# Attention of a hybrid backbone: where the norm's sums, the direct group and the last output products stand in the order

## The chip, the cores and the metric

The kernel runs on one core of one Trainium2 chip. The metric is device microseconds per execution; lower is better. Before the change, three runs gave 2841.94, 2845.85 and 2846.23 us, a median of 2845.85.

## The reference

The computation is a backbone of two layers over 1024 latent tokens and 256 context tokens of width 1024. Layer 0 mixes tokens by differential attention (8 heads, two score maps of 64 dimensions each, values of 128), layer 1 by a bidirectional state-space layer. Every mixer is followed by a squared-ReLU MLP of width 4096. All in float32. The change lies in the attention:

```python
def attend(q, k, v):
    s = jnp.einsum('bqhcd,bkhcd->bhcqk', q, k).astype(jnp.float32)
    p = jax.nn.softmax(s, axis=-1)
    w = p[:, :, 0] - lam * p[:, :, 1]
    o = jnp.einsum('bhqk,bkhe->bqhe', w.astype(v.dtype), v)
    return rmsnorm(o, subln_g) * (1.0 - lambda_init)
...
y_lat = jnp.einsum('bte,ed->btd', o_l, w_o)
```

Latent queries read all 1280 keys, context queries only the 256 context keys.

## The kernel before

**Number format.** A float32 product is made of three matmuls of rounded halves (hi·hi, hi·lo, lo·hi: `mm3`, L132, L133, L134). An operand is split by ScalarE (ACT), which writes the rounded hi half (L137), and by VectorE (DVE) or GpSimd (POOL), which writes the rest, lo (L138).

**Units.** Attention is the function `phase_b`. It runs 8 heads of 9 units, n = 9·head + u, and then a tail of five steps, n = 72 to 76. Unit u = 0 holds the 256 context queries, units 1 to 8 hold 128 latent queries each. Two latent units form a pair; the context unit is pair 0, so a head has five pairs, 0 to 4. A unit's scores wait for one another in this chain: scores on PE (L579, 18 matmuls), the two maps' maxima with a copy out of PSUM on DVE (L592), two exponentials on ACT (L602), and the combination of the two maps on DVE (L610, L611, L613). In the following unit the combined weights are transposed on PE in three parts (L625; L620 behind a context unit) and split, either straight from PSUM (`w_direct`: ACT L631 for hi, DVE L632 for lo) or by way of a copy (`w_copy`: ACT L638, then POOL L641 and L642). When a pair is complete, PE multiplies its weights with the values, ACT copies the result out (L732), POOL squares it (L733), and PE sums the squares over the head's 128 dimensions with a column of ones (`pair_sums`, L740); ACT copies the sums (L741).

**Fills.** Beside this chain PE has the projections of the next head's queries and keys. A group of them is eight products of three matmuls into bank 7 (in head 7, six products of the output matrix W_o). The table `FILLS` says how many stand ahead of the unit's first transposes, behind them, and behind the combination. Groups end either directly (ACT L523, DVE L524: hi and lo out of PSUM) or with the rotary embedding (ACT L528, DVE L529, POOL L534, DVE L537, and a split). In unit 2 the group has a direct end only, in the rows called `now`.

**PSUM.** There are eight banks of 512 columns. Scores of the first map take columns 0 to 1279 (banks 0, 1 and half of 2), of the second 1792 to 3071 (from the last quarter of bank 3 to bank 5). Columns 1280 to 1791, halves of banks 2 and 3, are called `whole` and take transposes. Bank 6 is `pb`: its lower half takes the values' products, its upper half (`high`) or the whole (`low`) takes transposes. Bank 7 takes the fills.

**Norms.** The sums of heads 0 to 6 are made into factors one head later (L746 to L748 on DVE, a transpose of the factors L760 to columns 1280 to 1407, L774 on DVE). Head 7 has no head behind it, so each of its pairs is normed by itself (`norm7`): factors on DVE and POOL (L746 to L748, L144), a diagonal matrix on POOL (L810), its broadcast by a matmul with ones (L814), a multiplication on DVE (L816) and a split. The steps of `norm7` are taken up at the ends of the two units behind the sums.

**W_o.** The output's first 512 columns for all ten token tiles start inside head 7 and the tail: a group takes six of the eight slices k of the contraction and is stored to `wod` in HBM (L857 copies it from PSUM). The last two slices, k = 6 and 7, of seven tiles are taken at n = 74, in the banks of the table `WO_BANKS`; later DVE adds them to what comes back from `wod` (L1453). The weights of these slices are split by `wsplit6(3)`: ACT L137 and POOL L138 of 1024 columns.

**What sets the order.** In `phase_b` the order on PE, DVE, ACT and POOL is the order in which the program writes the instructions (`manual`). SyncE's queue (SP) issues the loads and stores. What follows attention (the rest of W_o in `phase_c`, the MLP, layer 1) is ordered by a scheduler that lists the instructions by its own estimates, and is listed anew for a changed program.

Of the kernel before, what the change touches and what calls it, by code (L numbers as in the profile page):

```python
# [70 lines left out]
class Prog:  # L71
# [581 lines left out]
    FILLS = {0: (0, 3, 5, 8), 1: (0, 0, 0, 8), 2: (0, 2, 8, 8)}  # L653
# [28 lines left out]
    def phase_b(self):  # L682
# [24 lines left out]
        pb = self.bank(6)  # L707
# [29 lines left out]
        def pair_sums(h, pair):  # L737
            b = pb[:, 0:2] if h == 7 and pair > 2 else self.PS[:, 1790:1792]
            for i in range(2):
                mm(b[:, i : i + 1], sq[:, 128 * i : 128 * i + 128], self.ones, start=True, stop=True)  # L740
            nc.scalar.activation(hst[:, 1, h, 2 * pair : 2 * pair + 2], b, AF.Copy)  # L741
# [60 lines left out]
        def norm7(pair):  # L802
            b = pb[:, 256:512]
            newton = norm_calc(7, 2 * pair, 2 * pair + 2)
            g, c0 = cols7[pair]
# [55 lines left out]

        wo_at = dict(zip((63, 64, 65, 66, 68, 69, 70, 71, 72, 73), [8, 9] + list(range(8))))
# [15 lines left out]
        with self.manual():  # L878
            for n in range(72 + 5):
                h, u = units[n] if n < 72 else (8, 9)  # L880
                front = n < 72
                groups = []
# [24 lines left out]
                if groups:  # L907
                    a = self.FILLS.get(u, (0, 1, 5, 8) if n < 63 else (0, 0, 4, 6) if late else (0, 1, 4, 6))
                    if n > 71:
                        a = (0, 2, 4, 6) if n == 72 else (0, 4, 6, 6)  # L910
                    fills = [groups[0][0][a[i] : a[i + 1]] for i in range(3)]
# [69 lines left out]
                else:  # L981
# [14 lines left out]
                    w1 = part(1, last[:, 256:512] if pv and h < 7 else self.bank(0)[:, 0:256] if n == 72 else high)  # L996
# [5 lines left out]
                    now = groups and n < 63 and len(groups[0][1]) == 1  # L1002
                    if now:
                        groups[0][1][0]()
# [8 lines left out]
                if split:  # L1013
                    split()
                todo7, run7 = run7, []
# [23 lines left out]
                if n in (58, 61, 62, 70):  # L1039
                    wsplit6((58, 61, 62, 70).index(n))  # L1040
# [5 lines left out]
                if n == 74:  # L1046
                    for i, j in self.WO_BANKS.items():
                        g = 2 if i > 7 else i // 4
                        c0 = 128 * (i - self.G_TILES[g][0])
                        for k in (6, 7):  # L1050
                            hh, hl = (t[:, k, c0 : c0 + 128] for t in self.oT[g])
                            self.mm3(self.bank(j), hh, hl, wt6[k][0], wt6[k][1], k == 6, k == 7)
# [1593 lines left out]
```

## Time and profile before

| quantity | value |
| --- | --- |
| runs | 2841.94, 2845.85, 2846.23 us |
| profiled execution: time | 2845.55 us |
| profiled execution: span | 2843.8 us |
| PE busy | 2713.8 us, 95% of the span |
| DVE busy | 2025.9 us, 71% |
| ACT busy | 1368.1 us, 48% |
| POOL busy | 978.9 us, 34% |
| attention (`phase_b`) | 219 to 881 us of the span |

Times in rows of the profile are microseconds from the span's start, unless they are marked as ns. A row of the timeline gives the start, the duration, the engine, the line, the operation, the written and read buffers, their shapes, the count of equal instructions that follow one another, and, in brackets, how long the engine was idle before it and whose end it waited for. A row of the groups gives the same for all instructions of a line: the busy time, the mean of one in ns, then the idle time before them with what ended it.

### The profile page before, as it was taken

What the parts mean: (1) busy time and instruction counts of PE and PEld (TensorE: products, weight loads), DVE (VectorE), ACT (ScalarE), POOL (GpSimd) and SP (SyncE); (2) the same over time, 40 slices, a digit from 0 to 9 for tenths busy, and PEclk for the clock granted to TensorE, in tenths of its full rate; (3) what the DMA queues carried; (4) which work ended last, traced back from release to release, by engine and by line L of the source; (5) the groups of instructions that cost most, each with busy time, mean ns of one, the idle gap of its engine ahead of it and who ended that gap; (6) DMA issues with size and microseconds to landing.
All of it is one profiled execution on the core that took longest, in us unless ns stands there. A gap on an engine that the chain in (4) does not pass through costs nothing. (4 is left out here: it accounts for less than half of the span.)

```text
span 2843.8 us, 43784 instructions
## 1 busy us (share of the span) xinstructions
PE 2713.8 (95%) x15645; PEld 2259.5 (79%) x15645; DVE 2025.9 (71%) x3024; ACT 1368.1 (48%) x2584; POOL 978.9 (34%) x822
## 2 busy tenths in 40 slices
PE   5999999999999999999999999789999999999999
PEld 4688888888777787788877788788887778888887
DVE  6367888888773676767798877899543697668466
ACT  3425556666553753333444445477444633344443
POOL 3314555566553600000030013688121143335414
PEclk9999999999999999999999999899999999999999
DMA  9944233333515358886799877579642244477544
GB/s 273 322 170 138 62 89 92 94 91 110 167 58 175 130 186 313 296 308 215 258 312 304 279 232 260 171 231 307 229 163 89 71 161 159 154 246 228 167 132 141
DMA packets 377448, 539.13 MB, mean 190 GB/s; under 512 B 38287, under 2 KB 231053, under 8 KB 374029
## 3 DMA queue, kind: packets, MB, share of 16 engines
q1 hardware_dynamic: 377228, 536.32, 58.1%
q8 instruction: 123, 2.02, 0.3%
q14 instruction: 97, 0.79, 0.1%
HBM read 367.54 MB, written 164.47 MB: 187 GB/s over the span
## 5 line engine op out<-in xcount | busy, mean ns | idle before, releaser
L132 PE MATMUL PS<-H 128*128 128x512 f32 x1072 | 421.0, 394 | 2.5 <-ACT H L137 1.8
L134 PE MATMUL PS<-H 128*128 128x512 f32 x1072 | 418.0, 391 | 2.9 <-DVE H L138 1.6
L133 PE MATMUL PS<-H 128*128 128x512 f32 x1072 | 418.1, 390 | 0.0
L132 PE MATMUL PS<-H,R 128*128 128x512 f32 (+1 forms) x828 | 308.2, 374 | 12.5 <-DVE R L524 9.0
L133 PE MATMUL PS<-H,R 128*128 128x512 f32 (+1 forms) x828 | 299.1, 361 | 0.0
L134 PE MATMUL PS<-H,R 128*128 128x512 f32 (+1 forms) x828 | 298.3, 361 | 0.0
L132 PEld LDWEIGHTS PS<-H 128*128 128x128 f32 x1072 | 201.3, 188 | 50.3 <-issue 6.2
L134 PEld LDWEIGHTS PS<-H 128*128 128x128 f32 x1072 | 201.3, 188 | 46.0 <-DVE H L138 2.4
L133 PEld LDWEIGHTS PS<-H 128*128 128x128 f32 x1072 | 201.4, 188 | 40.4
L132 PE MATMUL PS<-R,H 128*128 128x512 f32 x534 | 213.7, 401 | 5.3 <-ACT H L137 3.3
L137 ACT ACTIVATE R<-W 128x512 fp32r<-128x512 f32 (+1 forms) x185 | 129.6, 708 | 179.1 <-PE PS L133 104.9
L137 ACT ACTIVATE H<-U 128x640 fp32r<-128x640 f32 x216 | 131.9, 675 | 173.2 <-PE PS L133 145.1
L133 PE MATMUL PS<-R,H 128*128 128x512 f32 x534 | 210.8, 395 | 2.8 <-POOL R L138 2.8
L134 PE MATMUL PS<-R,H 128*128 128x512 f32 x534 | 211.4, 397 | 1.8 <-DVE H L138 1.8
L602 ACT ACTIVATE F<-F,stat 128x1280 f32<-128x1280 f32 x128 | 174.3, 1362 | 80.3 <-DVE F L592 80.3
L592 DVE TENSOR_SCALAR_CACHE_REDUCE F<-PS 128x1280 f32<-128x1280 f32 x128 | 185.2, 1483 | 22.5 <-PE PS L579 22.5
L138 DVE TENSOR_TENSOR H<-U,H 128x640 fp32r<-128x640 f32 x216 | 162.2, 785 | 50.9 <-ACT H L137 50.6
L138 DVE TENSOR_TENSOR H<-W,H 128x512 fp32r<-128x512 f32 (+1 forms) x137 | 124.5, 919 | 102.0 <-ACT H L137 101.5
L132 PEld LDWEIGHTS PS<-H,R 128*128 128x128 f32 x828 | 157.6, 191 | 42.5 <-DVE R L524 10.4
L137 ACT ACTIVATE H<-W 128x512 fp32r<-128x512 f32 (+2 forms) x158 | 95.2, 613 | 186.3 <-PE PS L133 121.5
L134 PEld LDWEIGHTS PS<-H,R 128*128 128x128 f32 x828 | 157.4, 190 | 25.1 <-issue 0.8
L133 PEld LDWEIGHTS PS<-H,R 128*128 128x128 f32 x828 | 157.8, 191 | 19.8
(530 smaller groups left out, 6708.1 us busy)
## 6 DMA issues: line engine op xcount, KB each, us to landing
W<-in_mlp_w SPq DMA_DIRECT2D x176, 256.0 KB, 3.4
U<-Aa SPq DMA_DIRECT2D x108, 320.0 KB, 4.4
Aa<-FU SPq DMA_DIRECT2D x91, 320.0 KB, 4.7
Ad<-F SPq DMA_DIRECT2D x112, 256.0 KB, 2.9
W<-Ad SPq DMA_DIRECT2D x112, 256.0 KB, 2.7
FU<-in_mlp_w SPq DMA_DIRECT2D x32, 512.0 KB, 6.1
Ta<-FU SPq DMA_DIRECT2D x16, 1024.0 KB
U<-in_ada_w SPq DMA_DIRECT2D x32, 512.0 KB, 9.8
```

What stands on the lines that cost most here:

```text
L132: mm(out, ah, bh, start=first, stop=False, **kw)
L133: mm(out, ah, bl, start=False, stop=False, **kw)
L134: mm(out, al, bh, start=False, stop=last, **kw)
L137: self.nc.scalar.activation(hi, src, AF.Copy)
L138: (lo_eng or self.nc.vector).tensor_tensor(lo, src, hi.bitcast(F32), ALU.subtract)
L592: ts(p[c], self.PS[:, 1792 * c : 1792 * c + 1280], 1.0, None, ALU.mult, ALU.min, accum_out=sm[:, c : c + 1])
L602: nc.scalar.activation(p[c], p[c], AF.Exp, bias=sm[:, c : c + 1], scale=-1.0, accum_out=sn[:, 0:1] if c else s0[:, u + 1 : u + 2])
```

## The change

Six places are rewritten. None adds or removes an instruction on an engine.

1. The fills' table: in unit 0 four products (before, three) stand ahead of the first transposes and two behind them; unit 3 gets a row of its own, with two products ahead of them and five behind. In head 7, units 0 takes 4, 0 and 2 of W_o's six products, and units 3 to 8 have 2, 2 and 2 (or 0, 4 and 2) for 1, 3 and 2 (or 0, 4 and 2).
2. The sums of pair 4, which are made in unit 1 of the next head, go to columns 0 and 1 of bank 6, not to the last two columns of `whole` in bank 3.
3. In unit 2 the direct end of the projection group stands ahead of the copied part and the combination, not behind them. The unit's second part of transposes goes to the upper half of bank 6 and not to that of bank 7.
4. The broadcasts of head 7's norms for pairs 0 to 2 go to columns 1280 to 1535 (bank 2), not to the upper half of bank 6.
5. `wsplit6(3)` is called at n = 72, not at n = 70.
6. The 42 matmuls of W_o's last two slices, all together at n = 74 before, are dealt out by `wo_last`: tiles 8 and 9 ahead of pair 3's norm, 0 and 1 behind it, 2 at n = 75, and 3 and 4 behind pair 4's norm at n = 76.

```diff
-    FILLS = {0: (0, 3, 5, 8), 1: (0, 0, 0, 8), 2: (0, 2, 8, 8)}
+    FILLS = {0: (0, 4, 6, 8), 1: (0, 0, 0, 8), 2: (0, 2, 8, 8), 3: (0, 2, 7, 8)}
...
         def pair_sums(h, pair):
-            b = pb[:, 0:2] if h == 7 and pair > 2 else self.PS[:, 1790:1792]
+            b = pb[:, 0:2] if pair == 4 or h == 7 and pair > 2 else self.PS[:, 1790:1792]
...
         def norm7(pair):
-            b = pb[:, 256:512]
+            b = pb[:, 256:512] if pair > 2 else self.PS[:, 1280:1536]
...
+        def wo_last(*tiles):
+            for i in tiles:
+                g, b = 2 if i > 7 else i // 4, self.bank(self.WO_BANKS[i])
+                c0 = 128 * (i - self.G_TILES[g][0])
+                for k in (6, 7):
+                    hh, hl = (t[:, k, c0 : c0 + 128] for t in self.oT[g])
+                    self.mm3(b, hh, hl, wt6[k][0], wt6[k][1], k == 6, k == 7)
...
-                    a = self.FILLS.get(u, (0, 1, 5, 8) if n < 63 else (0, 0, 4, 6) if late else (0, 1, 4, 6))
+                    if n < 63 or 0 < u < 3:
+                        a = self.FILLS.get(u, (0, 1, 5, 8))
+                    else:
+                        a = (0, 4, 4, 6) if u == 0 else (0, 0, 4, 6) if late else (0, 2, 4, 6)
...
-                    w1 = part(1, last[:, 256:512] if pv and h < 7 else self.bank(0)[:, 0:256] if n == 72 else high)
+                    w1 = part(1, self.bank(0)[:, 0:256] if n == 72 else high)
+                    now = groups and n < 63 and len(groups[0][1]) == 1
+                    if now:
+                        groups[0][1][0]()
                     copied(w2)
                     if front:
                         self.combine(u, p, s0, sn)
                     fill(2)
                     direct(w1)
-                    now = groups and n < 63 and len(groups[0][1]) == 1
-                    if now:
-                        groups[0][1][0]()
                     next_post()
...
+                if n == 74:
+                    wo_last(8, 9)
                 todo7, run7 = run7, []
...
-                if n in (58, 61, 62, 70):
-                    wsplit6((58, 61, 62, 70).index(n))
+                if n in (58, 61, 62, 72):
+                    wsplit6((58, 61, 62, 72).index(n))
...
-                if n == 74:
-                    for i, j in self.WO_BANKS.items():
-                        g = 2 if i > 7 else i // 4
-                        c0 = 128 * (i - self.G_TILES[g][0])
-                        for k in (6, 7):
-                            hh, hl = (t[:, k, c0 : c0 + 128] for t in self.oT[g])
-                            self.mm3(self.bank(j), hh, hl, wt6[k][0], wt6[k][1], k == 6, k == 7)
+                if 74 <= n < 77:
+                    wo_last(*((0, 1), (2,), (3, 4))[n - 74])
```

Behind the diff the changed file's line numbers are 8 higher than those of before (L1453 is L1461 there).

How the order moves is shown at three places. The first is DVE in unit 2 of a middle head: L610, L611 and L613 are the combination, L632 the lo half of the second part of transposes, L524 the direct group's lo half. Before:

```order
L537 TENSOR_TENSOR FC<-FC 128x512
L610 RECIPROCAL stat<-stat 128x1
L611 SCALAR_TENSOR_TENSOR stat<-FC,stat,lamc 128x1
L613 SCALAR_TENSOR_TENSOR F_1851<-F_1851,stat 128x1280
L632 TENSOR_TENSOR R_110<-PS,R_110 128x2x128
L524 SCALAR_TENSOR_TENSOR R_110<-PS,R_1850 128x256
L138 TENSOR_TENSOR R_1850<-FC,R_1850 128x512
```

and after:

```order
L537 TENSOR_TENSOR FC<-FC 128x512
L524 SCALAR_TENSOR_TENSOR R_110<-PS,R_1850 128x256
L610 RECIPROCAL stat<-stat 128x1
L611 SCALAR_TENSOR_TENSOR stat<-FC,stat,lamc 128x1
L613 SCALAR_TENSOR_TENSOR F_1851<-F_1851,stat 128x1280
L632 TENSOR_TENSOR R_110<-PS,R_110 128x2x128
L138 TENSOR_TENSOR R_1850<-FC,R_1850 128x512
```

L524 has moved ahead of the combination; ACT's L523 moves in the same way.

The second place is POOL between unit 7 of head 7 and the tail; the L138 that writes 128x1024 is the lo half of `wsplit6(3)`, L733 the squares of a pair. Before:

```order
L138 TENSOR_TENSOR H<-FC,H 128x256
L138 TENSOR_TENSOR R_110<-W,R_110 128x1024
L138 TENSOR_TENSOR H<-W,H 128x256 x2
L733 TENSOR_TENSOR adat<-FC 128x256
L641 TENSOR_SCALAR R_110<-F_1851 128x2x128
```

and where it stands after:

```order
L641 TENSOR_SCALAR R_110<-F_1851 128x4x128
L642 TENSOR_TENSOR R_110<-F_1851,R_110 128x4x128
L138 TENSOR_TENSOR H<-FC,H 128x256
L138 TENSOR_TENSOR R_110<-W,R_110 128x1024
L733 TENSOR_TENSOR adat<-FC 128x256
L144 TENSOR_TENSOR FC<-FC,mhalf 128x2
```

It stands one pair later, ahead of pair 3's squares.

The third place is DVE in the tail; the two L816 are those of pairs 3 and 4, L1453 (after: L1461) adds a tile of W_o to what was stored. Before:

```order
L816 SCALAR_TENSOR_TENSOR FC<-FC,lamc,PS 128x256
L746 TENSOR_TENSOR FC<-FC 128x2
L747 TENSOR_SCALAR FC<-FC 128x2
L748 SCALAR_TENSOR_TENSOR FC<-FC 128x2
L1453 TENSOR_TENSOR FB<-FB,PS 128x512 x6
L816 SCALAR_TENSOR_TENSOR FC<-FC,lamc,PS 128x256
L138 TENSOR_TENSOR RT<-W,RT 128x1024
```

and after:

```order
L1461 TENSOR_TENSOR FB<-FB,PS 128x512 x2
L816 SCALAR_TENSOR_TENSOR FC<-FC,lamc,PS 128x256
L746 TENSOR_TENSOR FC<-FC 128x2
L747 TENSOR_SCALAR FC<-FC 128x2
L748 SCALAR_TENSOR_TENSOR FC<-FC 128x2
L1461 TENSOR_TENSOR FB<-FB,PS 128x512 x3
L816 SCALAR_TENSOR_TENSOR FC<-FC,lamc,PS 128x256
L1461 TENSOR_TENSOR FB<-FB,PS 128x512
L138 TENSOR_TENSOR RT<-W,RT 128x1024
```

Two of the additions now stand ahead of pair 3's L816, and one behind pair 4's.

The scheduler's order changes from there to the start of the MLP and is the same again behind it. In that stretch the transposes that make the MLP's features (L333, evacuated by L336 on ACT or L338 on DVE, split by L137 and L138) stand 2 to 5 us of PE's work later than before, measured in the products that stand ahead of them, while the products themselves keep their places.

## The prediction

> **What bounds the kernel now.** I read the page first, where PE is by far the busiest engine, then the windows table of the attention stretch, then the costliest groups of PE with the releaser of their idle time, and last the timeline around each wait. The change touches the hand-ordered attention (219 to 881 us) and, through the scheduler, the start of what follows. Columns of the windows row: stretch, length, busy us of PE, PEld, DVE, ACT, POOL with counts, granted TensorE clock, DMA share, GB/s.
>
> ```profile
> 219.00:881.00 662.00, 623.24 (x4338) 533.99 (x4336) 527.32 (x854) 377.23 (x759) 366.48 (x336) 0.98 0.33 100
> ```
>
> PE is idle for 662.00 − 623.24 = 38.8 us of the attention stretch. No product is removed by the change, so these 38.8 us, and matmuls that run at a lowered clock, are the ceiling of what it can give there. DVE, with 527 us, is the next engine, and waits on it are what PE's groups name:
>
> ```profile
> L740 PE MATMUL PS<-lamc,adat 128*128 128x1 f32 x160 | 21.1, 236 | 7.3 <-DVE R L632 7.3
> ...
> L132 PE MATMUL PS<-H,R 128*128 128x512 f32 (+1 forms) x828 | 308.2, 374 | 12.5 <-DVE R L524 9.0 <-ACT R L137 2.2 <-DVE FU L1680 0.8
> ...
> L625 PE MATMUL PS<-ident,F 128*128 128x128 f32 x640 | 95.1, 276 | 7.8 <-DVE F L613 4.2 <-DVE F L592 1.8 <-DVE R L632 1.4
> ```
>
> The norm's sums (L740) wait 7.3 us for L632, the projection products 9.0 us for L524. Those are the two waits that the first two edits address.
>
> **The sums in the values' bank.** Head 4 stands for heads 1 to 6, whose units run alike. In unit 1:
>
> ```profile
> 542.03 0.68 DVE L632 TENSOR_TENSOR R<-PS,R 128x512 fp32r<-128x512 f32 x1
> 542.85 0.58 PE L740 MATMUL PS<-lamc,adat 128*128 128x1 f32 x4 [1.24 <-DVE R L632]
> 543.36 2.02 PE L579 MATMUL PS<-R 64*128 64x512 f32 x18
> ```
>
> L740 writes bank 3, from which L632 still reads. In bank 6 nothing reads any more at that time, so L740 can follow the last product. What is late next: the scores L579 write the rest of L632's region only with their last third, some 1.4 us after their start, so L632's end (542.71) covers itself. I take off 1.37 us per head (the 1.24 of idle time plus the 0.13 by which a matmul that waited starts later than its neighbours' pitch of about 0.1), six heads: **−8.2**. Bounds 7.3 (the groups' idle alone) to 8.2.
>
> **The direct group emptied first.** Unit 2 and the first product of unit 3:
>
> ```profile
> 550.70 1.55 DVE L613 SCALAR_TENSOR_TENSOR F<-F,stat 128x1280 f32<-128x1280 f32 x1
> 552.17 0.42 DVE L632 TENSOR_TENSOR R<-PS,R 128x256 fp32r<-128x256 f32 x1
> 552.62 0.38 ACT L523 ACTIVATE R<-PS 128x256 fp32r<-128x256 f32 x1 [1.65 <-DVE R L632]
> 553.03 0.43 DVE L524 SCALAR_TENSOR_TENSOR R<-PS,R 128x256 fp32r<-128x256 f32 x1 [0.45 <-ACT R L523]
> 553.51 0.50 PE L132 MATMUL PS<-H,R 128*128 128x512 f32 x1 [1.32 <-DVE R L524]
> ```
>
> L523 and L524 go ahead of L613. PE's wait of 1.32 goes, 1.57 with the late start behind it, in seven heads: 11.0 if nothing else binds. But L613 now stands behind L524. I set its delay at 0.65: L524's 0.43 and half of the 0.45 by which that waits for L523. Then L613 starts at 551.35, L632 follows and ends 0.08 less than 0.42 after 552.90, at 553.25, where DVE is through at 553.46 today: DVE gains 0.2, not 1.57; what it gains is part of the 0.45 of waiting. In unit 4:
>
> ```profile
> 562.17 0.69 DVE L529 SCALAR_TENSOR_TENSOR FC<-PS,W 128x512 f32<-128x512 f32 x1 [0.45 <-ACT FC L528]
> 563.59 1.49 DVE L592 TENSOR_SCALAR_CACHE_REDUCE F<-PS 128x1280 f32<-128x1280 f32 x1
> ...
> 568.89 1.82 DVE L613 SCALAR_TENSOR_TENSOR F<-F,stat 128x1280 f32<-128x1280 f32 x1
> ...
> 570.86 0.63 PE L625 MATMUL PS<-ident,F 128*128 128x128 f32 x4
> ```
>
> L528 depends on PE and comes earlier, so the 0.45 ahead of L529 goes as well, and L592 of unit 4 comes 0.2 + 0.45, about 0.7, earlier. Its combination L613 ends 0.7 earlier, and unit 5's transposes L625, which today start 0.15 after it without idle time, now wait for it: PE keeps 0.7 of its 1.57. Six heads by 0.7 are 4.2; in head 0, where no earlier head's norm is on DVE, I give 1.2. **−5.4**, bounds 0 (all of it stands again before unit 5) and −11.0.
>
> **The table of fills.** Unit 0 gets a fourth product ahead of its transposes, unit 3 a second; these are meant to give DVE time, but the chain through DVE sets the pace:
>
> ```profile
> 527.14 0.63 PE L625 MATMUL PS<-ident,F 128*128 128x128 f32 x4 [0.60 <-DVE F L613]
> ...
> 536.76 1.48 DVE L592 TENSOR_SCALAR_CACHE_REDUCE F<-PS 128x1280 f32<-128x1280 f32 x1
> 537.81 0.93 PE L620 MATMUL PS<-ident,F 128*128 128x128 f32 x4
> ```
>
> Unit 0's 0.60 of waiting is filled by the product, which puts PE some 0.7 ahead. It then meets L592 in unit 1: four undisturbed transposes take 0.63, these four take 0.93, because the last two write bank 3 beside the scores that L592 reads until 538.24. An earlier PE waits there longer. **0**, bounds 0 to −4.2 (0.7 in six heads). [...]
>
> In unit 0 of head 7 the products are W_o's:
>
> ```profile
> 760.80 0.50 PE L132 MATMUL PS<-R,H 128*128 128x512 f32 x1 [1.24 <-ACT R L137]
> ...
> 764.14 0.80 PE L133 MATMUL PS<-R,H 128*128 128x512 f32 x1 [2.84 <-POOL R L138]
> 765.16 1.49 PE L625 MATMUL PS<-ident,F 128*128 128x128 f32 x6
> ```
>
> The product that waits 2.84 for POOL's split moves behind the six transposes. They, 1.49 us at a lowered clock, run inside the wait: **−1.3**, bounds 0 and −1.5.
>
> **Head 7's norms.** L814 of pairs 0 to 2 moves to bank 2, and POOL's 1024-wide split from unit 7 to the unit after the last scores.
>
> ```profile
> 814.35 0.67 PE L814 MATMUL PS<-FC 128*128 128x256 f32 x2 [1.13 <-POOL FC L144]
> ...
> 835.30 0.42 DVE L632 TENSOR_TENSOR R<-PS,R 128x256 fp32r<-128x256 f32 x1
> 835.87 0.67 PE L814 MATMUL PS<-FC 128*128 128x256 f32 x2 [1.31 <-POOL R L641]
> 838.53 2.40 POOL L138 TENSOR_TENSOR R<-W,R 128x1024 fp32r<-128x1024 f32 x1
> 838.55 2.41 DVE L747 TENSOR_SCALAR FC<-FC 128x2 f32<-128x2 f32 x1
> ...
> 843.11 0.44 PE L625 MATMUL PS<-ident,F 128*128 128x128 f32 x2 [0.84 <-DVE F L592]
> 844.52 0.67 PE L625 MATMUL PS<-ident,F 128*128 128x128 f32 x4 [0.97 <-DVE F L592]
> ...
> 869.28 0.17 DVE L747 TENSOR_SCALAR FC<-FC 128x2 f32<-128x2 f32 x1
> ```
>
> Pair 0: the columns that L814 takes now are the ones that the next transpose of norms uses, and that one has to wait for the norm's reader: 0, bounds 0 and −1.1. Pair 1: the row names L641, which has no part in these banks; L632, which reads bank 6, ends at 835.72, 0.15 ahead of L814, as L632 ended 0.14 ahead of L740 in unit 1. In bank 2 the 1.31 goes. Beside POOL's 2.40 us split the tiny L747 takes 2.41 where it takes 0.17 without it, which holds back the maxima; with the split gone, 0.84 + 0.97 of waiting go. After these waits the clock was low:
>
> ```profile
> 845.00:849.00 4.00, 4.00 (x13) 3.17 (x12) 2.94 (x5) 1.99 (x5) 2.45 (x3) 0.57 0.00 0
> ```
>
> The maxima come 2.41 − 0.17 = 2.24 earlier. PE would gain 1.31 + 0.84 + 0.97 = 3.12; the 0.88 between the two is a new wait of it on DVE in unit 8, so 2.24 is what arrives. At a granted 0.57 the 4 us hold 2.3 us of work at full speed: with the gaps gone I count the 1.7 as avoided. **−3.9**, bounds −1.3 (pair 1's wait alone) and −4.8 (3.12 + 1.7). The moved split costs 2.4 of POOL after the last scores, in POOL's idle time between pair 2's norm and pair 3's squares: 0; without that idle time 2.4 would reach pair 3's norm.
>
> **The tail.** The columns are start, duration, engine and so on as above.
>
> ```profile
> 867.96 0.70 PE L814 MATMUL PS<-FC 128*128 128x256 f32 x2 [0.87 <-POOL FC L810]
> ...
> 871.45 0.69 DVE L1453 TENSOR_TENSOR FB<-FB,PS 128x512 f32<-128x512 f32 x1 [0.62 <-PE PS L134]
> 873.27 0.69 DVE L1453 TENSOR_TENSOR FB<-FB,PS 128x512 f32<-128x512 f32 x1 [1.14 <-DMA FB<-wod]
> 871.23 0.72 POOL L810 TENSOR_SCALAR FC<-ident,FC 128x128 f32<-128x128 f32 x2
> ...
> 878.05 0.59 PE L814 MATMUL PS<-FC 128*128 128x256 f32 x2
> 878.68 0.48 DVE L816 SCALAR_TENSOR_TENSOR FC<-FC,lamc,PS 128x256 f32<-128x256 f32 x1 [1.10 <-PE PS L814]
> ...
> 881.56 1.70 PE L132 MATMUL PS<-RT,H 128*128 128x512 f32 x4 [2.92 <-ACT RT L137]
> ```
>
> Today two waits are open: 0.87 ahead of pair 3's broadcast and 2.92 after pair 4's, while its norm is multiplied and split. With tiles 8 and 9 ahead of the first and 3 and 4 behind the second, both are covered in part. What is new: pair 3's L816 stands on DVE behind two additions of tiles 8 and 9, which need their loads. Tile 9's addition doesn't wait for its load at 871.45, the next one does, until 873.27. The 12 matmuls end near 869.8, so pair 3's L816 starts between 870.6 and 871.5, where it can start at 868.7 today, when L814 is done. From there to the end of pair 4's diagonals (871.95) it takes 3.3 today: they come at 874 to 875 now. The last two tiles (12 matmuls, 2.8) and pair 4's broadcast then end at about 878.3, and the split weights, which follow pair 4's norm (3.5 us from L814 to the product today), let the next product start at about 879.45: 881.56 − 879.45, **−2.1**; bounds −1 and −3.8 (0.87 + 2.92).
>
> **What the scheduler did after it.** From 881 us on its order puts the transposes of the MLP's features 2 to 5 us of PE work later, the products staying. The waits there:
>
> ```profile
> L333 PE MATMUL PS<-ident,FB 128*128 128x128 f32 x44 | 7.5, 283 | 7.2 <-ACT FA L336 3.5 <-ACT FB L1420 2.0 <-DVE FA L338 1.6
> ...
> L138 POOL TENSOR_TENSOR H<-FA,H 128x256 fp32r<-128x256 f32 (+1 forms) x13 | 15.1, 1173 | 0.1
> ```
>
> Later transposes wait less of these 7.2, but their splits are nearer to the products that read them. I take **−1.5**, bounds −6 and +6.
>
> **Sum.** −8.2 − 5.4 + 0 − 1.3 − 3.9 − 2.1 − 1.5 = −22.4. The profiled execution took 2845.55 (span 2843.8), 0.3 less than the median of 2845.85; I predict 2845.55 − 22.4 = 2823.1. Its own range, with unit 3's wait, head 7 and the replan each moved by half of the way to a bound, is 2817 to 2831.
>
> **Rivals.**
> First, DVE doesn't bind: the whole 11.0 of unit 3 arrives (5.6 more) and the fills' 4.2. For it: DVE is busy 527 of 662 us, so there is room. Against it: its work sits in a chain with ACT's exponentials, and L592's hold on bank 3 shows in the 0.93. It gives 2823.1 − 9.8 = 2813.3. Chance 0.15.
>
> Second, the waits only move: unit 3's wait stands again before unit 5 (5.4 less), the tail's new DVE queue takes its 2.1, the replan gives nothing (1.5). For it: L625 already waits 4.2 us for L613; against it: DVE has 0.45 us of waits in these units to give up. That is 2823.1 + 9.0, 2832.1. Chance 0.20.
>
> Third, slower: the replanned feature steps. A transpose (0.28), its evacuation, and POOL's low half (1.17, one after another) make a chain; 16 steps of two groups now start later, and if the products run into each of them, every step costs at least 0.28 + 1.17 = 1.45 plus evacuation and high half. With 1.85 per step (16 × 1.85 = 29.6, less the 7.2 of waits that it takes the place of) the rest's −20.9 is used up; with 2.6 it is 41.6 − 7.2 − 20.9 = +13.5, 2859. Against it: POOL's idle time before these splits is 0.1, yet PE lost only 7.2 us there, so products have had other work to do. Chance 0.04.
>
> Fourth, the change is not to be told from none (0.2% is 5.7 us, about what a measurement of this kernel can tell): the gain of unit 1's sums goes to the next hand-over of the same head, as the second rival has it for unit 3, and only head 7's edits remain: 2832.1 + 8.2 = 2840.3. Against it: unit 1's sums have no reader of their bank left to wait for. Chance 0.06.
>
> The forecast has 0.55. The range that holds 8 in 10 takes in the first rival with its tail's and replan's better bounds (2813.3 − 1.7 − 2.5) and the second with some of the replan's worse one (2832.1 + 4): **2809 to 2836**. Faster by over 0.2%: all but the third and fourth and a little beside them, 0.91; the same 0.05; slower 0.04.
>
> **What would show it.** In the profile after: L740's idle time named L632 gone (a new releaser there means the second or fourth case); L524 no longer ahead of PE's idle time, and L613 naming L625 in unit 5 for about 0.9 us per head; if that is absent, DVE didn't bind. Unit 0's transposes waiting still less and unit 1's L620 longer. L747 at 0.17 and a full clock around 845. Pair 3's L816 behind tile 9's addition. The attention stretch (to the first product behind pair 4's norm) shorter by about 21 us, and the L333 waits smaller; if the stretch is 10 us shorter or less, steps one and two were wrong.

## The result

The changed kernel takes 2841.42 us (median of 11 runs, 2837.94 to 2843.45) against 2846.12 us of the kernel before (11 runs): a ratio of 0.9981, 95% interval 0.9972 to 0.9990, some 5 us faster. Predicted were 2823.1, 2809 to 2836. The sign was right, and less than a quarter of the gain came.

The profiled execution of the changed kernel took 2837.94 us (span 2836.2), 3.5 below its median, so stretches are compared here, not spans. Part of the spans' difference of 7.6 lies where both programs are the same: attention's first scores come 1.9 us earlier, and what follows the table's last stretch, nearly two thirds of the span, is 2.4 shorter. What the change can have moved is three stretches:

| stretch | before | after | difference |
| --- | --- | --- | --- |
| first scores to the scores of head 7's unit 8 | 617.03 | 611.07 | −5.96 |
| from there to the first product behind pair 4's norm | 45.09 | 42.84 | −2.25 |
| from there to a product in the MLP, at 1031.51 us before and 1026.25 after (W_o's rest, start of the MLP) | 149.95 | 154.79 | +4.84 |

Not all of the 5.96 is the change's: unit 2 of head 3 is 1.51 shorter, because the profile before has 3.41 us there at a granted clock of 0.50 (466.2 to 469.6) and the one after has none.

The costliest groups of PE after the change, in the same columns as before (busy, mean ns, idle time before them and its releasers):

```profile
L740 PE MATMUL PS<-lamc,adat 128*128 128x1 f32 x160 | 21.7, 240 | 2.6 <-ACT F L638 2.5
...
L132 PE MATMUL PS<-H,R 128*128 128x512 f32 (+1 forms) x828 | 307.8, 374 | 2.7 <-ACT R L137 2.1 <-ACT H L137 0.6
...
L625 PE MATMUL PS<-ident,F 128*128 128x128 f32 x640 | 92.9, 274 | 13.6 <-DVE R L632 10.2 <-DVE F L592 1.6 <-DVE F L613 0.9
...
L579 PE MATMUL PS<-R 64*128 64x512 f32 (+1 forms) x1216 | 139.2, 365 | 2.9 <-ACT F L638 2.3 <-issue 0.6
```

Both waits that the change was aimed at are gone: L740 has 7.3 us less for L632, the products 9.0 less for L524. But the transposes L625 now wait 10.2 us for L632 where they waited 1.4, the sums wait 2.5 for ACT's copy L638, and the scores 2.3. The scores' row before, the only one of the four that has not been shown, was

```profile
L579 PE MATMUL PS<-R 64*128 64x512 f32 (+1 forms) x1216 | 138.5, 367 | 0.7 <-ACT F L638 0.7
```

so the four groups' idle time falls from 28.3 us (7.3 + 12.5 + 7.8 + 0.7) to 21.8 (2.6 + 2.7 + 13.6 + 2.9), though 16.3 us of it was removed where the change meant to.

Head 4 shows where. The table has the length of a unit from the start of its scores to the next unit's, in us, in all profiled kernels that bear on it (units 2, 4, 6, 7 and 8 are the same within 0.04 everywhere):

| kernel | unit 0 | unit 1 | unit 3 | unit 5 |
| --- | --- | --- | --- | --- |
| before | 8.88 | 11.19 | 11.10 | 9.31 |
| after | 8.27 | 10.34 | 11.02 | 10.06 |
| sums alone | 8.87 | 9.71 | 11.14 | 9.27 |
| after, edit 3 undone | 8.27 | 10.33 | 10.63 | 9.78 |
| after, no POOL split in unit 2 | 8.27 | 10.32 | 11.20 | 9.38 |
| after, emptied between | 8.27 | 10.32 | 10.22 | 10.07 |
| the same, L774 earlier | 8.27 | 10.33 | 9.74 | 9.37 |
| after, order as before, bank 6 | 8.26 | 10.33 | 10.23 | 10.10 |

Units 0 and 1 give 1.46 per head, where 1.37 were forecast; unit 3, which was to give 1.57, gives 0.08; and unit 5 is 0.75 longer.

What happens in units 2 and 3 stands in the timeline after, first DVE and POOL, then PE:

```profile
544.73 0.42 DVE L524 SCALAR_TENSOR_TENSOR R<-PS,R 128x256 fp32r<-128x256 f32 x1 [0.33 <-ACT R L523]
...
545.26 0.65 DVE L611 SCALAR_TENSOR_TENSOR stat<-FC,stat,lamc 128x1 f32<-128x1 f32 x1
545.94 2.68 DVE L613 SCALAR_TENSOR_TENSOR F<-F,stat 128x1280 f32<-128x1280 f32 x1
548.55 0.41 DVE L632 TENSOR_TENSOR R<-PS,R 128x256 fp32r<-128x256 f32 x1
...
545.28 0.63 POOL L641 TENSOR_SCALAR R<-F 128x512 fp32r<-128x512 f32 x1 [3.61 <-ACT F L638]
545.99 1.29 POOL L642 TENSOR_TENSOR R<-F,R 128x512 fp32r<-128x512 f32 x1
...
549.01 0.66 PE L625 MATMUL PS<-ident,F 128*128 128x128 f32 x4 [1.04 <-DVE R L632]
```

Before, L613 took 1.55 and began at 550.70; POOL's split of the third part began just behind it:

```profile
550.79 1.94 POOL L641 TENSOR_SCALAR R<-F 128x512 fp32r<-128x512 f32 x1 [3.32 <-ACT F L638]
552.81 1.28 POOL L642 TENSOR_TENSOR R<-F,R 128x512 fp32r<-128x512 f32 x1
```

There L613 came first and POOL's L641 took 1.94 instead of its 0.63. Now L524 stands ahead, the combination comes later, POOL is first, L611 takes 0.65 instead of 0.22 and L613 2.68 instead of 1.55: it ends 1.34 after L642 does (547.28), which is nearly its whole own length. DVE ends its combination 2.2 us later in the unit, and L632 behind it is what unit 3's transposes, in the same bank 6, wait for. Unit 5 is then late as foreseen, and by more. The trace names no wait for L613 there, but the transposes L625 start 0.15 behind its end (563.80 + 1.82 = 565.62), as they did before:

```profile
564.13 0.62 PE L579 MATMUL PS<-R 64*128 64x256 f32 x6 [0.25 <-ACT F L638]
565.77 0.63 PE L625 MATMUL PS<-ident,F 128*128 128x128 f32 x4
```

The last scores of unit 5 come 0.53 later than their pitch, the transposes 0.29.

### The profile page after: what moved, and what is told of

It reads as the page before. It is cut to its first block, busy times and chain, and to the rows that moved or that the text cites. A ratio compares the mean times of both kernels' runs of the same rounds, so it can differ in the third digit from the quotient of the medians.

```text
span 2836.2 us, 43788 instructions
## 1 busy us (share of the span) xinstructions
PE 2717.2 (96%) x15645; PEld 2257.1 (80%) x15645; DVE 2035.5 (72%) x3024; ACT 1368.5 (48%) x2584; POOL 973.1 (34%) x822
## 5 line engine op out<-in xcount | busy, mean ns | idle before, releaser
L137 ACT ACTIVATE H<-U 128x640 fp32r<-128x640 f32 x216 | 131.9, 674 | 171.8 <-PE PS L133 147.0
L137 ACT ACTIVATE R<-W 128x512 fp32r<-128x512 f32 (+1 forms) x185 | 129.6, 708 | 175.8 <-PE PS L133 107.1
L592 DVE TENSOR_SCALAR_CACHE_REDUCE F<-PS 128x1280 f32<-128x1280 f32 x128 | 185.1, 1482 | 20.4 <-PE PS L579 20.4
L138 DVE TENSOR_TENSOR H<-U,H 128x640 fp32r<-128x640 f32 x216 | 164.1, 793 | 49.4 <-ACT H L137 46.8
L138 DVE TENSOR_TENSOR H<-W,H 128x512 fp32r<-128x512 f32 (+1 forms) x137 | 126.0, 930 | 102.5 <-ACT H L137 101.9
L137 ACT ACTIVATE H<-W 128x512 fp32r<-128x512 f32 (+2 forms) x158 | 95.6, 613 | 188.9 <-PE PS L133 118.2
L132 PEld LDWEIGHTS PS<-H,R 128*128 128x128 f32 x828 | 157.4, 190 | 31.9 <-issue 4.1
L134 PEld LDWEIGHTS PS<-H,R 128*128 128x128 f32 x828 | 157.2, 190 | 25.1 <-issue 0.8
L138 DVE TENSOR_TENSOR R<-W,R 128x512 fp32r<-128x512 f32 (+1 forms) x149 | 138.4, 936 | 49.0 <-ACT R L137 47.1
```

The lines of the kernel that those rows point to most:

```text
L132: mm(out, ah, bh, start=first, stop=False, **kw)
L134: mm(out, al, bh, start=False, stop=last, **kw)
L137: self.nc.scalar.activation(hi, src, AF.Copy)
L138: (lo_eng or self.nc.vector).tensor_tensor(lo, src, hi.bitcast(F32), ALU.subtract)
L592: ts(p[c], self.PS[:, 1792 * c : 1792 * c + 1280], 1.0, None, ALU.mult, ALU.min, accum_out=sm[:, c : c + 1])
```

## The experiments

All ratios are to the kernel before, run beside the kernel on the same chip.

**Edit 2 alone.** The kernel before with

```diff
-            b = pb[:, 0:2] if h == 7 and pair > 2 else self.PS[:, 1790:1792]
+            b = pb[:, 0:2] if pair == 4 or h == 7 and pair > 2 else self.PS[:, 1790:1792]
```

> The kernel before with edit 2 alone: pair 4's sums in bank 6. Theory (each edit is worth what its own unit shows): unit 1 is 1.37 us shorter in heads 1 to 6 and nothing later is longer, so 8.2 us less than before, some 0.9971. Rival (a wait that goes comes back at the next hand-over of the head): unit 1 shorter, units 3 or 5 longer by about as much, the time within 2 us of before.

2836.59 us, ratio 0.9968 (0.9955 to 0.9982), 9.2 less. In its groups,

```profile
L740 PE MATMUL PS<-lamc,adat 128*128 128x1 f32 x160 | 20.6, 232 | 0.0
```

the sums wait for nothing, and unit 1 is 1.48 shorter in heads 2 to 6 (1.38 in head 1). The other units of heads 1 to 6 are within 0.05 of before but for three: unit 2 of head 3, which is 1.51 shorter without before's half clock, unit 3 behind it (0.36 longer), and unit 7 of head 6 (2.78 longer, with 3.41 us of half clock of its own from 733.0). The theory holds. By the medians this one line gave more than the whole change, though the two intervals overlap.

**Edit 3 undone.** In unit 2 the group is emptied behind the combination again, and the second part goes to bank 7; the rest is as changed.

```diff
-                    w1 = part(1, self.bank(0)[:, 0:256] if n == 72 else high)
-                    now = groups and n < 63 and len(groups[0][1]) == 1
-                    if now:
-                        groups[0][1][0]()
+                    w1 = part(1, last[:, 256:512] if pv and h < 7 else self.bank(0)[:, 0:256] if n == 72 else high)
                     copied(w2)
                     if front:
                         self.combine(u, p, s0, sn)
                     fill(2)
                     direct(w1)
+                    now = groups and n < 63 and len(groups[0][1]) == 1
+                    if now:
+                        groups[0][1][0]()
```

> The changed kernel with edit 3 undone: in unit 2 the group is emptied behind the combination again, and the second part of transposes is in bank 7. Theory (edit 3 costs more than it gives, since the combination it delays now runs beside POOL's split): unit 3 has its wait of about 1.5 for L524 again, but the waits of 1.2 and 0.5 behind it go, and unit 5's 0.8 goes; 0.7 to 0.8 per head in six heads, 4.5 us less than the changed kernel. Rival (the prediction's: edit 3 gives 5.4): 5 us more than the changed kernel, about the time of before less 0.5.

2835.46 us, ratio 0.9961 (0.9948 to 0.9975): some 6 us less than the changed kernel. Edit 3 is a loss. Against the sums alone the rows of the table show one thing more: the fourth product in unit 0 makes it 0.60 shorter, and unit 1 gives back 0.62, where the last two transposes now wait for DVE's maxima:

```profile
535.84 0.44 PE L620 MATMUL PS<-ident,F 128*128 128x128 f32 x2 [0.34 <-DVE F L592]
```

The second product ahead in unit 3 makes that 0.51 shorter, and unit 5 gives back 0.51. The table of fills is worth 0, as predicted.

**POOL's part in unit 2 taken away.** The third part is split from PSUM by ACT and DVE behind the combination.

```diff
-                    copied(w2)
+                    if not now:
+                        copied(w2)
                     if front:
                         self.combine(u, p, s0, sn)
+                    if now:
+                        direct(w2)
```

> The changed kernel, but in unit 2 the third part of transposes is split straight from PSUM by ACT and DVE behind the combination, not by way of ACT's copy and POOL (L641, L642). DVE has 0.69 more to do there, POOL nothing. Theory (DVE's combination waits for POOL's split): L613 of unit 2 back from 2.7 to 1.55 and L611 from 0.65 to 0.22, 1.56 less than after, so that even with the 0.69 L632 of the second part ends some 0.9 earlier, and the wait of unit 3's transposes is 0.2 or less instead of 1.2; 5 to 8 us less than the changed kernel. Rival (the wait is the order's and the bank's own, POOL has no part in it): L613 stays near 2.7, the transposes wait 1.2 or, with the added 0.69, 1.9; the changed kernel's time or up to 4 us more.

2840.91 us, ratio 0.9979 (0.9970 to 0.9989): the changed kernel's time. The theory was right on DVE and wrong on the price:

```profile
549.74 1.55 DVE L613 SCALAR_TENSOR_TENSOR F<-F,stat 128x1280 f32<-128x1280 f32 x1
...
551.94 0.63 PE L579 MATMUL PS<-R 64*128 64x256 f32 x6 [1.70 <-DVE R L632]
```

Without POOL beside it L613 is back at 1.55 and L611 at 0.22. But the third part lies in `whole`, and until DVE has read it unit 3's last scores wait 1.70, a wait that ACT's copy of it (L638, 0.60 in the changed kernel) had kept away.

**Emptied between the combination and the second part.** On DVE, L524 behind L613 and ahead of L632; on ACT as in the change.

```diff
-                    if now:
-                        groups[0][1][0]()
-                    copied(w2)
+                    if not now:
+                        copied(w2)
                     if front:
                         self.combine(u, p, s0, sn)
+                    if now:
+                        groups[0][1][0]()
+                        copied(w2)
```

> The changed kernel, but in unit 2 the group is emptied between the combination and the second part's low half (on ACT ahead of the copy, as in the changed kernel; on DVE behind L613). Theory (who comes first, L613 or POOL's L641, decides): L613 starts before L641 and takes 1.55, L641 waits instead; L524 ends some 0.9 later than in the changed kernel, and unit 3's first product waits about 0.4 for it, its transposes for nothing. Unit 3 is about 1 us shorter than in the changed kernel, unit 5 0.8: 8 to 10 us less than the changed kernel in six heads. Rival (the start's order doesn't matter, only that both engines work): L613 is again about 2.7, and the time is that of the changed kernel or above.

2834.81 us, ratio 0.9960 (0.9946 to 0.9974), 6 us less than the changed kernel, where 8 to 10 were expected. Unit 3 is 0.8 shorter, unit 5 not at all. The timeline says why:

```profile
543.81 1.55 DVE L613 SCALAR_TENSOR_TENSOR F<-F,stat 128x1280 f32<-128x1280 f32 x1
...
546.54 1.51 DVE L774 SCALAR_TENSOR_TENSOR W<-W,lamc 128x256 f32<-128x256 f32 x1
547.97 1.48 DVE L592 TENSOR_SCALAR_CACHE_REDUCE F<-PS 128x1280 f32<-128x1280 f32 x1
...
544.17 1.67 POOL L641 TENSOR_SCALAR R<-F 128x512 fp32r<-128x512 f32 x1 [3.61 <-ACT F L638]
545.92 1.85 POOL L642 TENSOR_TENSOR R<-F,R 128x512 fp32r<-128x512 f32 x1
```

L613 starts 0.36 before L641 and takes 1.55, and L641 takes 1.67 instead of 0.63: here the one that starts first keeps its length, as expected. But POOL's L642 is then pushed onto L774, which takes 1.51 instead of 0.47. DVE's maxima of unit 3 begin 11.51 us after unit 2's start, against 11.60 before and 12.31 after: PE gained, DVE did not, and unit 5 collects the difference.

**L774 moved as well.** The same kernel, with the multiplication of the earlier head's norm ahead of the first part's low half, where DVE waits 0.60 for ACT.

```diff
+                    early = groups and n < 63 and len(groups[0][1]) == 1
+                    if early:
+                        split = norm()
                     direct(w0)
                     next_post()
...
-                    split = norm()
+                    if not early:
+                        split = norm()
```

> The kernel of the run before (the group emptied between the combination and the second part's low half), with the multiplication of the earlier head's norm (L774) moved in unit 2 from behind the combination to ahead of the first part's low half, where DVE waits 0.6 for ACT. Theory (DVE's chain from unit 2 to unit 5 sets the pace, and its collisions with POOL's splits are part of it): L774 takes 0.47 and not 1.51, DVE's maxima of units 3 and 4 come about 1.4 earlier, unit 5's 0.8 of waiting goes; 0.7 to 0.9 per head in six heads, 4 to 5 us less than that kernel, about 2830. Rival (unit 5 waits for something else, or POOL's instruction then hits the next one on DVE): unit 5 still 10.0 long, time within 1 us of that kernel.

2829.07 us, ratio 0.9944 (0.9931 to 0.9958), 16 less than before and 5 to 6 less than the run above; expected were 4 to 5, about 2830.

```profile
541.28 0.48 DVE L774 SCALAR_TENSOR_TENSOR W<-W,lamc 128x256 f32<-128x256 f32 x1
...
546.49 1.48 DVE L592 TENSOR_SCALAR_CACHE_REDUCE F<-PS 128x1280 f32<-128x1280 f32 x1
```

L774 is 0.48 long, the maxima of unit 3 start 10.08 after unit 2's start, those of unit 4 18.96 (before 20.23), and unit 5 is back at 9.37. So the chain through DVE from unit 2 to unit 5 sets the pace of a head; PE's wait for L524 only showed it.

**The tail's edits alone.** The changed kernel with edits 2 and 3 and the table's rows for heads 0 to 6 undone:

```diff
-    FILLS = {0: (0, 4, 6, 8), 1: (0, 0, 0, 8), 2: (0, 2, 8, 8), 3: (0, 2, 7, 8)}
+    FILLS = {0: (0, 3, 5, 8), 1: (0, 0, 0, 8), 2: (0, 2, 8, 8)}
...
-            b = pb[:, 0:2] if pair == 4 or h == 7 and pair > 2 else self.PS[:, 1790:1792]
+            b = pb[:, 0:2] if h == 7 and pair > 2 else self.PS[:, 1790:1792]
```

> The changed kernel with edits 2 and 3 and the table's rows for heads 0 to 6 undone: only head 7's and the tail's edits are left. Theory (what the change's trace shows is theirs): unit 0 of head 7 2.4 shorter, unit 3 0.7 longer, unit 7 0.8 shorter, the first product behind the norms 2 to 3 earlier, which a load of W_o's next columns takes back (the second wait of these products 1.3 to 2.2 longer); the scheduler's part 0 to 3 worse; together 0 to 3.5 us less than before. Rival (the prediction's sizes): 7 to 9 us less than before.

2846.60 us, ratio 1.0007 (0.9996 to 1.0018): nothing. I had 8.8 for these edits with the scheduler's part. Unit 3 of head 7 is 0.7 longer and unit 7 0.8 shorter, as in the changed kernel. Unit 0, where I had 1.3, can't be told: it is 10.7 to 14.0 long in all the kernels, and unit 7 of head 6 is 9.7 to 12.6; even the kernel with the sums alone has 11.89 for unit 0 against 14.04 before. In the changed kernel the product's wait for POOL's split there falls from 2.84 to 1.26, but the transposes ahead of it now wait 2.39 for L632 (756.09), and the stretch at a granted 0.50 that begins in this unit is 6.83 us long instead of 10.24.

**The dealing undone.**

```diff
-                if n == 74:
-                    wo_last(8, 9)
...
-                if 74 <= n < 77:
-                    wo_last(*((0, 1), (2,), (3, 4))[n - 74])
+                if n == 74:
+                    wo_last(*self.WO_BANKS)
```

> The changed kernel with the last products of W_o all at n = 74 again (edit 6 undone). Theory (the gain of the dealing is taken back at the load of W_o's next columns): the first product behind the norms 2 to 3 us later after the last scores, the second wait for the split weights 0.2 instead of 1.2 to 2.2; the time within 1.5 us of the changed kernel, but for what the scheduler's order makes of it. Rival (the dealing keeps its gain): 2 to 3 us more than the changed kernel.

2838.79 us, ratio 0.9976 (0.9966 to 0.9987), beside the changed kernel's 0.9981: the dealing gives nothing in the end. It does its own work. The first product behind pair 4's norm starts 42.67 us after the last scores without it, 41.09 with it (before: 43.35). What takes it back stands in the changed kernel's timeline:

```profile
862.08 1.50 DVE L1461 TENSOR_TENSOR FB<-FB,PS 128x512 f32<-128x512 f32 x2 [10.62 <-DMA FB<-wod]
863.49 0.47 DVE L816 SCALAR_TENSOR_TENSOR FC<-FC,lamc,PS 128x256 f32<-128x256 f32 x1
...
871.46 1.45 PE L132 MATMUL PS<-RT,H 128*128 128x512 f32 x4 [1.21 <-ACT RT L137]
...
882.72 1.06 ACT L137 ACTIVATE RT<-W 128x1024 fp32r<-128x1024 f32 x1 [10.36 <-DMA W<-in_attn_w_o]
...
883.83 1.20 PE L132 MATMUL PS<-RT,H 128*128 128x512 f32 x4 [2.21 <-ACT RT L137]
```

Pair 3's L816 stands behind the additions that wait for their loads, as predicted, and the wait for the split weights falls from 2.92 to 1.21. Then PE reaches the next weights of W_o before their load is there and waits 2.21. The MLP's start is slower too. Eighty microseconds behind these products, first before, then after:

```profile
888.00:968.00 80.00, 71.90 (x350) 58.01 (x349) 34.37 (x36) 50.30 (x100) 49.62 (x63) 1.00 0.52 167
```

```profile
880.00:960.00 80.00, 68.28 (x316) 54.63 (x315) 31.40 (x34) 48.66 (x98) 49.66 (x62) 0.96 0.49 160
```

PE is busy 3.6 us less. Of the clocks, 1.00 and 0.96, half is the windows' choice: both kernels have 3.41 us at 0.50 just behind the norms, before from 882.6, ahead of its window, and after from 885.0, within it. The changed kernel has one such stretch more, from 953.3.

How much of this is the scheduler's order can be read from the other traces. Eight more kernels here have the changed kernel's order on PE, DVE, ACT and POOL from the first product behind the norms to the end of the table's third stretch: edit 3 undone, POOL's part taken away, emptied between, L774 moved, the tail's edits alone, and the three runs below on the split, on one product ahead and on bank 6. The stretch takes 150.5 to 152.8 us in them, against 154.8 in the changed kernel and 149.95 before; the wait of 2.21 for the load is 0.26 to 1.85 in them. With all the last products at n = 74, here and in the last run below, DVE, ACT and POOL have the order of before, and it takes 150.1 and 150.8. So it is the dealing that brings the new order, which is 0.5 to 2.8 us slower in eight profiles, and the rest of the 4.84 is not the order's alone. One wait stands in all nine kernels with that order, at 2.36 to 2.40, while no transpose L333 of this stretch waited over 1.64 before:

```profile
947.55 0.76 PE L333 MATMUL PS<-ident,FB 128*128 128x128 f32 x5 [2.37 <-DVE FA L338]
```

The kernel with the sums alone has a third order, on PE too, and takes 149.0.

**The 1024-wide split moved back.**

```diff
-                if n in (58, 61, 62, 72):
-                    wsplit6((58, 61, 62, 72).index(n))
+                if n in (58, 61, 62, 70):
+                    wsplit6((58, 61, 62, 70).index(n))
```

> The changed kernel with POOL's 1024-wide split back behind unit 7's end (edit 5 undone). Theory (DVE's instructions wait for whichever POOL instruction runs beside them; without this one others stand there): the stretch from unit 8's scores to its transposes 0 to 1 us longer, L747 or L795 at over 2 again, time within 1 us of the changed kernel. Rival (the prediction's: this split is what holds the maxima, 2.2 and the clock's 1.7): 2 to 4 us more than the changed kernel.

2841.50 us, ratio 0.9988 (0.9979 to 0.9997), within the interval of the changed kernel. The time is as the theory had it, but at its place the theory missed and the prediction's term held:

```profile
836.54 2.36 DVE L746 TENSOR_TENSOR FC<-FC 128x2 f32<-128x2 f32 x1
...
836.30 2.58 POOL L138 TENSOR_TENSOR R<-W,R 128x1024 fp32r<-128x1024 f32 x1
...
841.72 0.69 PE L625 MATMUL PS<-ident,F 128*128 128x128 f32 x2 [2.68 <-DVE F L592]
```

With the split there, the transposes wait 2.68; in the changed kernel 0.64:

```profile
829.62 2.38 DVE L795 SCALAR_TENSOR_TENSOR W<-W,lamc 128x256 f32<-128x256 f32 x2
...
835.06 0.44 PE L625 MATMUL PS<-ident,F 128*128 128x128 f32 x2 [0.64 <-DVE F L592]
836.48 0.66 PE L625 MATMUL PS<-ident,F 128*128 128x128 f32 x4 [0.97 <-DVE F L592]
```

So moving the split is worth 2.04 at this place. But it only made good what the edits beside it cost there: the two L795, 0.93 before, take 2.38 beside POOL's other work, and the combination of unit 7 is 0.7 later. Before the change the two waits were 0.84 and 0.97.

**One product ahead in units 3 and 7 of head 7.** The changed kernel with the old row there:

```diff
-                        a = (0, 4, 4, 6) if u == 0 else (0, 0, 4, 6) if late else (0, 2, 4, 6)
+                        a = (0, 4, 4, 6) if u == 0 else (0, 0, 4, 6) if late else (0, 1, 4, 6)
```

> The changed kernel with one product of W_o, as before, and not two, ahead of the transposes in head 7's units 3 and 7. Theory (the second product puts the transposes, ACT's first split and so the exponentials and the combination 0.7 later in both): unit 3 of head 7 7.8 long instead of 8.5 and its sums wait for nothing; in unit 7 the combination starts 7.15 behind the unit's start instead of 7.84, and the wait of unit 8's transposes of 0.8 shrinks below 0.3. Rival (the sums wait for the copy of the third part for another reason): unit 3 stays at 8.5.

One run, 2835.50 us, so only its profile is read. Unit 3 is 7.79 long (8.49) and its sums wait for nothing; unit 7 is 8.35 (9.02), and its combination starts 7.15 after its scores, not 7.84. The second product in front does cost 0.7 in both units: in these units ACT makes the transposes' first split ahead of the exponentials, so whatever delays the transposes delays the softmax. Unit 8's waits, 0.64 and 0.97, stayed as in the changed kernel, against the expectation, since PE came earlier by the same 0.7.

**The old order with bank 6.** Edit 3's order undone, its bank kept:

```diff
-                    now = groups and n < 63 and len(groups[0][1]) == 1
-                    if now:
-                        groups[0][1][0]()
                     copied(w2)
                     if front:
                         self.combine(u, p, s0, sn)
                     fill(2)
                     direct(w1)
+                    now = groups and n < 63 and len(groups[0][1]) == 1
+                    if now:
+                        groups[0][1][0]()
```

> The changed kernel with the group of unit 2 emptied behind the combination again, as before the change, but the second part of transposes still in bank 6. Theory (POOL's split beside the delayed combination makes unit 3's transposes wait, not the bank): L613 of unit 2 1.55 long; unit 3's first product waits 1.5 for L524, its transposes of bank 6 wait for nothing; unit 3 10.6, unit 5 9.8 long, as in the run with all of edit 3 undone. Rival (the bank is the cause): the transposes wait about 1.2 for L632 here too, and unit 3 is 11 or longer.

One run, 2831.80 us, so only its profile is read. Unit 3 is 10.23 long, shorter than after, and its transposes wait for nothing; its first wait is smaller than expected:

```profile
547.98 0.50 PE L132 MATMUL PS<-H,R 128*128 128x512 f32 x1 [0.81 <-DVE R L524]
```

The bank alone does not make the new wait: in the old order it is gone. L613 is 1.55 here and L774 1.51, as in the run with the group emptied between, and unit 5 is 10.10.

**What the runs speak for, together.** Edit 2, edits 4 and 5, the group emptied between with L774 ahead, the last products all at n = 74, one product ahead in units 3 and 7 of head 7: the diffs above.

> What the runs speak for, together: the sums in bank 6, in unit 2 the group emptied between the combination and the second part's low half and L774 ahead of the first part's, the norms of head 7 in bank 2, the split at n = 72, but the last products of W_o all at n = 74 as before, and in head 7's units 3 and 7 one product ahead of the transposes as before. Theory: 2829.1 (the run with L774 moved) less 2.6 (the dealing undone, as it measured on the changed kernel) less 0.7 each in units 3 and 7: 2825, range 2822 to 2829. Rival (the scheduler's part behind attention takes the difference back): 2829 to 2832.

2825.32 us (5 runs, 2824.93 to 2828.54), ratio 0.9935 (0.9919 to 0.9951): 19 us less than the kernel before, as expected (2825), and faster than both. Units 3 and 7 of head 7 are 7.80 and 8.35 long, as in the run for them. The waits left in its groups:

```profile
L132 PE MATMUL PS<-H,R 128*128 128x512 f32 (+1 forms) x828 | 307.5, 374 | 6.1 <-DVE R L524 2.8 <-ACT R L137 2.2 <-ACT H L137 1.0
...
L625 PE MATMUL PS<-ident,F 128*128 128x128 f32 x640 | 92.0, 274 | 6.5 <-DVE R L632 3.6 <-DVE F L592 1.6 <-DVE F L613 1.0
```

## Why the prediction was right or wrong

**Sums in bank 6, −8.2: right.** 1.48 per head in the profile, 9.2 in the runs of that edit alone. The prediction took a new releaser of L740 as a sign that the waits only move. L638 did come (2.5 us in the changed kernel), but at other pairs' sums, which stay in `whole`, and with edit 3; with the sums alone they wait for nothing.

**Direct group first, −5.4: wrong, and the step that carries the miss.** In the profile units 3 and 5 together are 0.67 longer per head, 4 us in six heads; undoing the edit gives 6. The step that failed is "I set its delay at 0.65 … L613 starts at 551.35": it moved a block of 1.55 on DVE by 0.65 and kept its length. Measured, the combination started 1.03 later in the unit and ended 2.2 later, because it then ran beside POOL's split instead of ahead of it. The maxima of unit 4, which I had 0.7 earlier, came 0.71 later. The prediction had the effect in its own rows (L747 at 2.41 beside POOL's split) and did not ask what POOL does where L613 was moved to. The part of the reasoning that was sound is what happens to a gain of PE that DVE does not share: it came back at unit 5, as the prediction said (0.82 of waits there, and in the run with the group emptied between, the same).

**The table of fills, 0: right in unit 0** (−0.60, and +0.62 in unit 1), by the wait of L620 that was forecast (behind L592, 2.6 us before and 5.2 after). No run shows the first rival's 4.2 for the fills: what unit 0 gains, unit 1 gives back. Not seen was the second product ahead of the transposes in units 3 and 7 of head 7, 0.7 each; the prediction looked at heads 0 to 6 alone.

**Head 7's norms and the split, −3.9: mis-sized.** From unit 7's start to unit 8's transposes 0.97 came. Pair 1's wait of 1.31 is gone, but 0.44 of it stands at the sums L740, which now wait for ACT's copy L638. L747's 2.24 did come (2.04), and L795 beside POOL and the later combination took as much back; L747, which was to be back at 0.17, took 0.67. The clock's 1.7 did not come here: four microseconds behind these transposes had 0.57 granted before, and after

```profile
836.90:840.90 4.00, 4.00 (x14) 3.17 (x12) 2.89 (x5) 2.04 (x5) 2.40 (x3) 0.57 0.00 0
```

Of the ten kernels here with the split at n = 72, all with waits of about 0.64 and 0.97 at these transposes, four have such a stretch behind them and six have none, so these waits do not decide it.

**The tail, −2.1: right at its place** (2.25 in the profile), and taken back from 12 us later on, by the load of W_o's next columns and by the new order behind it. The prediction did not follow the load: it ended at the first product.

**The scheduler's part, −1.5, bounds ±6: +0.5 to +2.8** in the eight other kernels of that order, against before, one profile each, within the bounds and on their bad side; the 4.84 of the changed kernel's own profile holds more than the order. The L333 waits did shrink, from 7.2 to 6.7 us, and it gave nothing; what else the order costs is open. Head 7, the tail and this part together, −8.8 in the prediction, gave nothing in the run of the tail's edits alone.

What came has the fourth rival's size (2840.3) by another way: the gain of the sums stayed, edit 3 cost the 4 to 6 us that the prediction had it give, and the rest gave nothing. Together that is −9.2 + 4 to 6, or −5 to −3, where −4.7 were measured. The second rival, that the waits only move, is nearest in kind, but it put unit 3 and the replan at 0, where they cost. No rival named POOL. The sign that the prediction named for its first two steps being wrong, an attention stretch shorter by 10 us or less, came (8.2), but only the second step was wrong.

## What to carry to other kernels

Before moving an instruction on DVE, look at what POOL does in the window it moves into, and take the instruction's length from rows of its line beside the same work: L613 took 1.55 with POOL idle and 2.68 beside L642. Where PE waits for an engine that is also the head's chain, taking the wait away on PE is worth only what that engine's chain gains; measure the chain (here the start of the maxima from unit to unit), not the wait. A gain at the end of one phase has to be followed to the next load that was issued at a fixed point of the program.

## What the runs showed of the hardware

In these rows some instructions of DVE and POOL take longer where the two run beside each other. L613 (128x1280) takes 1.55 when it starts 0.36 before POOL's L641 or when POOL is idle, and 2.68 beside L642; L641 takes 0.63 ahead of that L613 and 1.94 where it starts 0.09 behind an L613 of 1.55. It falls on tiny instructions as well: L746 on 128x2 elements took 2.36 beside a 2.58 us split, L747 2.41 beside one of 2.40 (at their shortest 0.15 and 0.17 in the kernel before). L592 and L632, which read PSUM, show no such stretching (L592 1.47 to 1.49; L632 0.41 to 0.42 on 128x256 and 0.68 to 0.69 on 128x512, in all kernels). By what the two engines hold each other up these runs do not show.

Starts that lie close together do not tell who holds. L613 started at 545.94, 0.05 before POOL's L642, in a break of 0.08 between two POOL instructions, and still ran 2.68. In the kernel with the group emptied between, DVE's L138 started at 545.94, 0.02 behind POOL's L642, and kept its 0.68, while L642 took 1.85 instead of 1.28.
